# A fixed order for the out-projection's products, transfers at 310 bytes a ns in the planner's table, and all splits on VectorE

## The chip, the cores and the metric

One core of a Trainium2 chip runs the whole program. The metric is device time in microseconds (us), less is better, as the median of several runs. TensorE (PE) multiplies into PSUM, VectorE (DVE), ScalarE (ACT) and GpSimd (POOL) do the rest, SyncE (SP) issues the transfers.

## The reference, cut to what matters

Two layers over 512 tokens of width 1024, in float32. Layer 0 uses stick-breaking attention, layer 1 forgetting attention; both end in a gated feed-forward part.

```python
# layer 0
a = rmsnorm(h, sb_pre_g)
q, k, v = jnp.split(a @ sb_w_qkv, 3, axis=-1)
o = stick_breaking_attention(q, k, v)              # 16 heads of 64
h = h + rmsnorm(merge_heads(o) @ sb_w_o, sb_post_g)    # out-projection
f = conv_ffn(rmsnorm(h, ffn_pre_g), w_up, conv_w, conv_b, w_down)
h = h + rmsnorm(f, ffn_post_g)
# layer 1: the same with forgetting_attention, w_kvf, fox_w_q, fox_w_o
```

`conv_ffn` multiplies by `w_up` (1024 x 5632), convolves three tokens deep, gates, and multiplies by `w_down` (2816 x 1024).

## The kernel before, in words

Every float32 product is made of three: each operand is split into a high part that TensorE takes as it is (`hi`, `AH`) and the rest (`lo`, `AL`), and `AH*hi`, `AH*lo` and `AL*hi` are added in PSUM. A weight tile arrives in `raw` (two buffers), ScalarE writes `whi` (L380) and VectorE `wlo = raw - whi` in two halves (L384); there are eight buffers of each. Three of the eight row tiles of each out-projection weight (`POOL_ROWS`) have their `wlo` made by GpSimd.

Attention goes through eight pairs of heads. A head's scores go to PSUM banks 0 to 2; in layer 0 ScalarE and VectorE then take an Exp (L666), a minimum (L667), two masks (L644, L646), a Ln (L669), a running sum (L670), an Exp (L671) and a product (L672). TensorE transposes the result (L680), ScalarE and VectorE split it into `PH` and `PL` (L686, L687), and TensorE multiplies it with V (L692). The sum goes into `oT` (L701, L702). When both heads of pair p are done, `AH[:, p]` (L720) and `AL[:, p]` (L721) are made of it, `AL` on GpSimd for p under 4 and on VectorE above.

The out-projection (`unit`, L733) has 32 units (b, k), of a block b of 128 tokens and a pair k, with six products each. Block 0 adds up in banks 4 and 5, block 1 in 0 and 1, block 2 in 2 and 3, block 3 in 6 and 7. Units with k = 7 need the last head of all. When a block is complete, `post_block` and `pre_block` normalise it (`mixed`): Square on ScalarE (L465), two small steps on GpSimd (L442, L443), a multiplication by a gain `g` and an update of H on VectorE (L466, L468), again Square (L449), the two small steps, the scaled copy `t` (L454), eight transposes on TensorE (L457), and the split into `AH` (L459) and `AL` (L460). Only then can the first product of the feed-forward part (L436) read that block; it takes tokens 0 to 255, so blocks 0 and 1, for its first three pairs of weight tiles, and the other half after that. At the start of the program `pre_block` does the same for the input.

The order on each engine isn't the order of the code. `Order.pin` records all instructions with what they depend on, `Order.schedule` walks through them by a table of costs (a list schedule: an engine that is free takes the ready instruction with the lowest rank), and the outcome is fixed with dependencies. The code gives an instruction's rank (its place in the program, less `AHEAD` where it reads or writes PSUM, plus `BEHIND` for the splits of weights), so TensorE's products of the out-projection go wherever the planner thinks that they are ready. A transfer in that table takes 520 ns to issue, 1300 ns to start, its bytes at 200 a ns on a wire that all share, and 800 ns to land. SyncE's own order is the program's.

## Time and profile before

| | us |
|---|---|
| median of 3 runs | 1281.49 (1281.36 to 1285.04) |
| the profiled execution's own time | 1283.62 |
| its span in the profile | 1281.8 |
| TensorE busy in the span | 1240.6 |
| VectorE, ScalarE, GpSimd busy | 812.4, 649.4, 103.5 |

The profile follows one execution. The 1.8 us between its own time and its span lie before the first and behind the last instruction. "Busy" is a sum over the whole span; the stretches in which TensorE waits, or gets a lower clock, are read from the rows below.

### The profile page before, as it was taken

The page shows a single profiled execution, that of the slowest core. Times are in us where ns is not written, and L with a number is a line of the kernel's source. Part 1 is how long each engine was busy: PE and PEld are TensorE (multiplying, and loading weights), DVE is VectorE, ACT ScalarE, POOL GpSimd, SP SyncE. Part 2 cuts the span into 40 slices and gives each one's busy share as a digit, 9 for nine tenths or more (in the row PEclk, how much of TensorE's full clock was granted, in tenths as well). Part 3 has the DMA queues.
Part 4 walks back from the last instruction along what each step waited for, and adds up shares of the span by engine and source line. Part 5 has one row for each costly group of instructions (what it writes and reads, how often), then busy time and mean ns, then how long its engine had stood idle before and what let it go on. Part 6 is the DMA issues. An engine that isn't in the chain of part 4 may idle for free.

```text
span 1281.8 us, 16749 instructions
## 1 busy us (share of the span) xinstructions
PE 1240.6 (97%) x6485; PEld 1061.9 (83%) x6485; DVE 812.4 (63%) x1304; ACT 649.4 (51%) x1085; POOL 103.5 (8%) x163
## 2 busy tenths in 40 slices
PE   6999999979999999999998999999899999999998
PEld 5898887869888888888897988978798888888886
DVE  5799999467655555433477888872775555554323
ACT  4688777445433333323477888772553333333221
POOL 1000003020000000000001221241200000000001
PEclk9999999989999999999999999999899999999999
DMA  5313222124433333333221122132343333333301
GB/s 171 98 51 102 79 67 66 50 66 135 129 99 99 99 95 94 93 98 99 66 69 50 34 66 75 58 99 66 99 134 114 99 95 93 95 97 99 99 33 66
DMA packets 145927, 111.97 MB, mean 87 GB/s; under 512 B 4680, under 2 KB 136120, under 8 KB 145848
## 3 DMA queue, kind: packets, MB, share of 16 engines
q1 hardware_dynamic: 145848, 110.90, 29.1%
q8 instruction: 51, 0.84, 0.3%
q14 instruction: 28, 0.23, 0.1%
HBM read 108.79 MB, written 2.10 MB: 87 GB/s over the span
## 4 chain that ended last, share of the span: by engine, by line
PE 86%; DVE 9%; ACT 2%; issue 2%; POOL 0%; DVEq 0%; POOLq 0%; ACTq 0%
PE PS L436 49%; PE PS L733 23%; PE PS L614 6%; PE PS L692 3%; PE PS L680 2%; PE PS L634 2%; DVE ec L670 1%; PE PS L457 1%; DVE wlo L384 1%; DVE PL L687 1%; DVE ec L672 1%; DVE t L454 1%; DVE QS L585 1%; DVE t L466 0%; DVE ec L667 0%
## 5 line engine op out<-in xcount | busy, mean ns | idle before, releaser
L436 PE MATMUL PS<-AH,whi 128*128 128x512 f32 (+1 forms) x1088 | 400.4, 368 | 5.8 <-DVE QS L585 3.1
L436 PE MATMUL PS<-AL,whi 128*128 128x512 f32 (+1 forms) x1088 | 400.9, 369 | 1.1 <-DVE AL L460 1.1
L436 PE MATMUL PS<-AH,wlo 128*128 128x512 f32 (+1 forms) x1088 | 400.1, 368 | 0.0
L384 DVE TENSOR_TENSOR wlo<-raw,whi 128x512 fp32r<-128x512 f32 x332 | 216.7, 690 | 211.4 <-ACT whi L380 210.9
L380 ACT CAST whi<-raw 128x1024 fp32r<-128x1024 f32 x172 | 180.1, 1050 | 197.5 <-PE PS L436 167.4
L436 PEld LDWEIGHTS PS<-AH,whi 128*128 128x128 f32 x1088 | 207.9, 191 | 37.7 <-DVE QS L585 3.2
L436 PEld LDWEIGHTS PS<-AL,whi 128*128 128x128 f32 x1088 | 207.8, 191 | 33.1 <-DVE AL L460 1.7
L436 PEld LDWEIGHTS PS<-AH,wlo 128*128 128x128 f32 x1088 | 207.6, 191 | 31.3
L794 DVE SCALAR_TENSOR_TENSOR hc<-PS,cw,hc 128x511 f32<-128x511 f32 (+1 forms) x176 | 131.3, 746 | 8.6 <-ACT hc L792 5.5
L733 PE MATMUL PS<-whi,ah 128*128 128x512 f32 x352 | 109.3, 390 | 0.0
L733 PE MATMUL PS<-whi,al 128*128 128x512 f32 x352 | 109.1, 389 | 0.0
L733 PE MATMUL PS<-wlo,ah 128*128 128x512 f32 x352 | 108.9, 389 | 0.0
L817 DVE TENSOR_TENSOR al<-act,ah 128x512 fp32r<-128x512 f32 x44 | 30.4, 691 | 116.6 <-ACT ah L816 116.6
L816 ACT CAST ah<-act 128x512 fp32r<-128x512 f32 x44 | 27.4, 623 | 146.2 <-PE PS L733 138.2
L733 PEld LDWEIGHTS PS<-whi,al 128*128 128x128 f32 x352 | 66.1, 188 | 13.7
L733 PEld LDWEIGHTS PS<-wlo,ah 128*128 128x128 f32 x352 | 66.1, 188 | 13.7
L733 PEld LDWEIGHTS PS<-whi,ah 128*128 128x128 f32 x352 | 65.9, 188 | 13.7
L614 PE MATMUL PS<-whi,AH 128*128 128x256 f32 x256 | 73.5, 288 | 3.1 <-ACT whi L380 3.1
L442 POOL TENSOR_SCALAR ss<-ss 128x1 f32<-128x1 f32 x31 | 12.0, 387 | 781.2 <-ACT junk L465 721.4
L614 PE MATMUL PS<-wlo,AH 128*128 128x256 f32 x256 | 73.9, 289 | 0.0
L614 PE MATMUL PS<-whi,AL 128*128 128x256 f32 x256 | 73.3, 287 | 0.0
L792 ACT ACTIVATE hc<-PS,cw 128x512 f32<-128x512 f32 x88 | 68.1, 774 | 8.4 <-PE PS L436 8.3
(132 smaller groups left out, 1740.7 us busy)
## 6 DMA issues: line engine op xcount, KB each, us to landing
raw<-w_up_dram SPq DMA_DIRECT2D x88, 512.0 KB, 3.8
raw<-w_down_dram SPq DMA_DIRECT2D x44, 512.0 KB, 3.6
raw<-sb_w_qkv_dram SPq DMA_DIRECT2D x24, 512.0 KB, 3.7
raw<-w_kvf_dram SPq DMA_DIRECT2D x16, 512.0 KB, 3.7
raw<-sb_w_o_dram SPq DMA_DIRECT2D x8, 512.0 KB, 3.5
raw<-fox_w_q_dram SPq DMA_DIRECT2D x8, 512.0 KB, 3.6
raw<-fox_w_o_dram SPq DMA_DIRECT2D x8, 512.0 KB, 3.6
H<-x_dram SPq DMA_DIRECT2D x4, 512.0 KB, 8.3
```

Source lines behind the costliest of these rows:

```text
L380: order.move(nc.scalar.copy(hi, raw), BEHIND)
L384: order.move(eng.tensor_tensor(out=fl[:, s], in0=fr[:, s], in1=fh[:, s], op=ALU.subtract), BEHIND)
L436: nc.tensor.matmul(ps, a[:, k, :m], b[:, k, t0:t1], start=i == 0, stop=i == n - 1)
L614: nc.tensor.matmul(ps[:, o], a[:, k, sl], m[:, k % 4, :], start=i == 0, stop=i == 3 * KT - 1)
L634: nc.tensor.matmul(z[:, ZOFF[b] : ZOFF[b] + n], a[:, b * P : (b + 1) * P], m[:, :n], start=i == 0, stop=i == len(passes) - 1,)
L680: nc.tensor.transpose(zt[:, o : o + P], E[:, ZOFF[b] + j * P : ZOFF[b] + (j + 1) * P], ident)
L692: nc.tensor.matmul(av[:, j * P :], V[:, j, hh, :], m[:, o : o + n], start=i == 0, stop=i == 7,)
L733: nc.tensor.matmul(y[:, c, :], s[:, sl], m[:, 0, c * 512 : (c + 1) * 512], start=k == 0 and i == 0, stop=k == n - 1 and i == 2,)
L792: nc.scalar.activation(hc, y[:, i, :], AF.Identity, scale=col[:, 2:3], bias=col[:, 3:4])
L794: nc.vector.scalar_tensor_tensor(out=hc[:, s:], in0=y[:, i, : T - s], scalar=col[:, 2 - s : 3 - s], in1=hc[:, s:], op0=ALU.mult, op1=ALU.add,)
L816: nc.scalar.copy(ah, act[:, k, :])
L817: nc.vector.tensor_tensor(out=al, in0=act[:, k, :], in1=f32(ah), op=ALU.subtract)
```

## The change: what it does

1. The out-projection's units get a fixed order by extra dependencies among TensorE's instructions (`Order.after`): units (0, 0..5), (1, 0..3), (0, 6), then (1, 4) no sooner than the last transpose of the last head, (1, 5) no sooner than its last product with V, then (1, 6), (1, 7), (0, 7), and then blocks 2 and 3 whole. Block 1 is complete before block 0. The units held to the end of the down-projection are chained in the same way.
2. The planner's table for a transfer: 310 bytes a ns in place of 200, 700 ns to land in place of 800; the start is 1300 as before.
3. `POOL_ROWS` is gone: VectorE makes every `wlo`, and every `AL` of an attention output.

```diff
-POOL_ROWS = (1, 5, 7)
+FILL = (4, 5)
...
-    ISSUE, FLIGHT, BYTES = 520, 2100, 200.0
+    ISSUE, LEAD, LAND, BYTES = 520, 1300, 700, 310.0
...
+    def after(self, later, earlier):
+        self.turns += [(b.ins.name, a.ins.name) for b in later for a in earlier]
...
+        at = {i.name: n for n, i in enumerate(prog)}
+        for b, a in self.turns:
+            preds[at[b]].setdefault(at[a], 2)
...
-                wire = max(wire, t + 1300) + done - self.FLIGHT
-                end = wire + 800
+                wire = max(wire, t + self.LEAD) + done
+                end = wire + self.LAND
...
-    stream += [row_tile(sb_w_o[0], k, nc.gpsimd if k in POOL_ROWS else nc.vector) for k in range(KT)]
+    stream += [row_tile(sb_w_o[0], k) for k in range(KT)]
...
-                (nc.gpsimd if p < 4 else nc.vector).tensor_tensor(
+                nc.vector.tensor_tensor(
...
-    def out_proj(done):
+    def out_proj(done, heads_end):
         w = {}
-        for b in range(NB):
-            for k in range(KT):
-                if k not in w:
-                    w[k] = take()
-                unit(b, k, KT, (AH[:, k, :], AL[:, k, :]), w[k])
-            done(b)
+        one = [(1, k) for k in range(KT)]
+        steps = [(0, k) for k in range(KT - 2)] + one[: FILL[0]] + [(0, KT - 2), heads_end[0]]
+        steps += one[FILL[0] : FILL[1]] + [heads_end[1]] + one[FILL[1] :]
+        steps += [(0, KT - 1)] + [(b, k) for b in (2, 3) for k in range(KT)]
+        before = []
+        for step in steps:
+            if not isinstance(step, tuple):
+                before.append(step)
+                continue
+            b, k = step
+            if k not in w:
+                w[k] = take()
+            mms = unit(b, k, KT, (AH[:, k, :], AL[:, k, :]), w[k])
+            order.after(mms, before)
+            before = mms[-1:]
+            if k == KT - 1:
+                done(b)
```

Since the planner lays out the whole program, other places move too. Lines 733, 721, 384, 454, 457 and 670 of the kernel before are 742, 730, 392, 462, 465 and 678 in the changed one. Three places:

**TensorE, the end of layer 0's out-projection, before.** `whi24` to `whi31` are the row tiles for k = 0 to 7; `t4` is the normalised block that is transposed. The six `whi31` products in a row are of blocks 0, 1 and 2, the last three rows ahead of the transposes are unit (3, 7):

```order
L733 MATMUL PS_67<-whi27_1819,AH_82 128x512 x2
L733 MATMUL PS_67<-wlo27_1820,AH_82 128x512
L733 MATMUL PS_67<-whi31_2240,AH_82 128x512 x6
L733 MATMUL PS_67<-wlo31_2241,AH_82 128x512
...
L733 MATMUL PS_67<-whi31_2240,AH_82 128x512 x2
L733 MATMUL PS_67<-wlo31_2241,AH_82 128x512 x2
L733 MATMUL PS_67<-whi31_2240,AL_83 128x512 x2
L457 MATMUL PS_67<-ident_68,t4_2343 128x128 x8
L457 MATMUL PS_67<-ident_68,t4_2413 128x128 x8
```

and the same end in the changed kernel: the first three rows are unit (0, 7), the fourth begins unit (2, 0); below the gap stand products of the units (2, 3) and (2, 4) with the transposes of block 1 among them:

```order
L742 MATMUL PS_67<-whi31_2240,AH_82 128x512 x2
L742 MATMUL PS_67<-wlo31_2241,AH_82 128x512 x2
L742 MATMUL PS_67<-whi31_2240,AL_83 128x512 x2
L742 MATMUL PS_67<-whi24_1553,AH_82 128x512 x2
...
L742 MATMUL PS_67<-whi27_1819,AL_83 128x512 x2
L742 MATMUL PS_67<-whi28_1826,AH_82 128x512 x2
L465 MATMUL PS_67<-ident_68,t4_2385 128x128 x8
L742 MATMUL PS_67<-wlo28_1827,AH_82 128x512 x2
```

Before, blocks 0, 1 and 2 become complete together, 27 products of block 3 ahead of the first transposes, with both first transposes at the very end. Now 32 products stand between the last one of block 1 and its transposes, 47 between the last of block 0 and its own, and the transposes of blocks 1, 0 and 2 stand among products of blocks 2 and 3. Layer 1 has the same rows with other numbers.

**VectorE, the last heads of layer 0, before**, from the second mask of head 13 (`ec_2069`, of 0 to 15) to the running sum of head 14 (`ec_2121`):

```order
L646 TENSOR_TENSOR ec_2069<-ec_2069,mask_a_73 128x128
L384 TENSOR_TENSOR wlo30_2026<-raw30_2024,whi30_2025 128x512 x2
L670 SCALAR_TENSOR_TENSOR ec_2070<-R_243,ec_2070 128x1280
L667 TENSOR_SCALAR ec_2120<-ec_2120 128x1280
L644 TENSOR_TENSOR ec_2120<-ec_2120,mask_a_73 128x3x128
L646 TENSOR_TENSOR ec_2120<-ec_2120,mask_a_73 128x128
L672 TENSOR_TENSOR ec_2069<-ec_2069,ec_2070 128x1280
L670 SCALAR_TENSOR_TENSOR ec_2121<-R_243,ec_2121 128x1280
```

and in the changed kernel:

```order
L654 TENSOR_TENSOR ec_2069<-ec_2069,mask_a_73 128x128
L730 TENSOR_TENSOR AL_83<-oT_236,AH_82 128x512
L710 TENSOR_TENSOR oT_236<-PS_67,ot_1984 64x512
L392 TENSOR_TENSOR wlo30_2026<-raw30_2024,whi30_2025 128x512
L678 SCALAR_TENSOR_TENSOR ec_2070<-R_243,ec_2070 128x1280
L675 TENSOR_SCALAR ec_2120<-ec_2120 128x1280
L652 TENSOR_TENSOR ec_2120<-ec_2120,mask_a_73 128x3x128
L654 TENSOR_TENSOR ec_2120<-ec_2120,mask_a_73 128x128
L730 TENSOR_TENSOR AL_83<-oT_236,AH_82 128x512
L680 TENSOR_TENSOR ec_2069<-ec_2069,ec_2070 128x1280
L678 SCALAR_TENSOR_TENSOR ec_2121<-R_243,ec_2121 128x1280
```

Two of the moved `AL` stand ahead of the running sum and of the product of head 13, and one half of `wlo30` has moved behind them.

**TensorE at the start of the program, before** (`whi0`, `wlo0` are the first weight tile, `t4_129` and `t4_145` the first two blocks of the input):

```order
L457 MATMUL PS_67<-ident_68,t4_129 128x128 x8
L614 MATMUL PS_67<-whi0_100,AH_82 128x256
L457 MATMUL PS_67<-ident_68,t4_145 128x128 x8
L614 MATMUL PS_67<-wlo0_101,AH_82 128x256
L614 MATMUL PS_67<-whi0_100,AL_83 128x256
```

and now:

```order
L465 MATMUL PS_67<-ident_68,t4_129 128x128 x8
L465 MATMUL PS_67<-ident_68,t4_145 128x128 x8
L622 MATMUL PS_67<-whi0_100,AH_82 128x256
L622 MATMUL PS_67<-wlo0_101,AH_82 128x256
L622 MATMUL PS_67<-whi0_100,AL_83 128x256
```

The transposes of the second block have moved ahead of the first product; on ScalarE the Square of the second block has moved ahead of the first block's split, and on VectorE the second `t` ahead of the first `AL`. SyncE's order is the same but for one swap of neighbours in each layer; the order within the feed-forward parts and at the end of the program is the same.

## Rows read from the trace of the kernel before

**Rows 1.** The page, part 1: busy us (share of the span) and instructions.
```profile
PE 1240.6 (97%) x6485; PEld 1061.9 (83%) x6485; DVE 812.4 (63%) x1304; ACT 649.4 (51%) x1085; POOL 103.5 (8%) x163
```

**Rows 2.** Waits of TensorE, whole span: us in total, times, longest.
```profile
PE PS L457 <- DVE t L454: 17.2, 5, 8.4
```

**Rows 3.** Timeline of TensorE, layer 0: start, us, instruction, [idle before, releaser].
```profile
268.91 1.06 PE L457 MATMUL PS<-ident,t 128*128 128x128 f32 x8 [0.46 <-DVE t L454]
274.87 1.97 PE L457 MATMUL PS<-ident,t 128*128 128x128 f32 x8 [4.90 <-DVE t L454]
277.94 0.79 PE L436 MATMUL PS<-AH,whi 128*128 128x256 f32 x2 [1.10 <-ACT AH L459]
279.20 0.58 PE L436 MATMUL PS<-AL,whi 128*128 128x256 f32 x1 [0.47 <-DVE AL L460]
```

**Rows 4.** Timeline of TensorE, the same place in layer 1.
```profile
906.88 1.09 PE L457 MATMUL PS<-ident,t 128*128 128x128 f32 x8 [2.64 <-DVE t L454]
909.07 0.78 PE L436 MATMUL PS<-AH,whi 128*128 128x256 f32 x2 [1.10 <-ACT AH L459]
910.53 0.58 PE L436 MATMUL PS<-AL,whi 128*128 128x256 f32 x1 [0.68 <-DVE AL L460]
```

**Rows 5.** Windows: length; busy of PE, PEld, DVE, ACT, POOL; PEclk, DMA share, GB/s.
```profile
225.00:230.00 5.00, 5.00 (x20) 4.58 (x19) 4.19 (x7) 3.66 (x6) 0.00 (x0) 0.51 0.00 0
275.00:280.00 5.00, 3.43 (x13) 2.74 (x14) 4.31 (x5) 3.03 (x5) 1.39 (x3) 0.50 0.34 100
280.00:285.00 5.00, 5.00 (x28) 5.00 (x27) 4.57 (x5) 1.08 (x3) 1.79 (x3) 0.55 0.62 177
910.00:915.00 5.00, 4.47 (x21) 4.47 (x21) 4.45 (x6) 2.63 (x5) 3.16 (x4) 0.50 0.35 104
```

**Rows 6.** Timelines of ScalarE and VectorE: block 0's first Square and its `t`.
```profile
261.51 1.02 ACT L465 ACTIVATE junk<-PS 128x1024 bf16<-128x1024 f32 x1 [5.57 <-PE PS L733]
267.48 1.28 DVE L454 SCALAR_TENSOR_TENSOR t<-H,ss,g 128x1024 f32<-128x1024 f32 x1 [2.19 <-POOL ss L443]
```

**Rows 7.** Chain of waits, merged pieces: start, us, what.
```profile
254.85 6.59 PE PS L733 x29
291.11 9.00 PE PS L436 x75
```

**Rows 8.** Timeline of VectorE in layer 0's last heads.
```profile
201.29 2.07 DVE L672 TENSOR_TENSOR ec<-ec 128x1280 f32<-128x1280 f32 x1 [0.18 <-ACT ec L671]
218.67 1.48 DVE L672 TENSOR_TENSOR ec<-ec 128x1280 f32<-128x1280 f32 x1
220.09 2.83 DVE L670 TENSOR_TENSOR_SCAN ec<-R,ec 128x1280 f32<-128x1280 bf16 x1
```

**Rows 9.** Timeline of GpSimd in layer 0's last heads.
```profile
201.97 6.72 POOL L721 TENSOR_TENSOR AL<-oT,AH 128x512 fp32r<-128x512 f32 x4
```

**Rows 10.** Line 721 on VectorE: count, ns min/median/max, first and last start.
```profile
L721 DVE TENSOR_TENSOR AL<-oT,AH x8: 681/693/1617, 205.9 to 878.0; 128x512 fp32r<-128x512 f32 x8
```

**Rows 11.** Timeline of TensorE in layer 0's last heads.
```profile
220.21 1.09 PE L680 MATMUL PS<-ident,ec 128*128 128x128 f32 x8 [0.89 <-DVE ec L672]
223.70 0.79 PE L692 MATMUL PS<-PL,V 128*128 128x512 f32 x1 [1.66 <-DVE PL L687]
```

**Rows 12.** Timelines of ScalarE and TensorE at the start of the program.
```profile
5.00 1.06 ACT L449 ACTIVATE junk<-H 128x1024 bf16<-128x1024 f32 x1 [2.94 <-DMA H<-x_dram]
10.44 1.01 ACT L459 CAST AH<-PS 128x1024 fp32r<-128x1024 f32 x1 [4.29 <-PE PS L457]
11.35 1.06 ACT L449 ACTIVATE junk<-H 128x1024 bf16<-128x1024 f32 x1
16.41 0.56 PE L614 MATMUL PS<-wlo,AH 128*128 128x256 f32 x1
```

**Rows 13.** The page, part 6: transfers, count, KB each, median us to landing.
```profile
raw<-w_up_dram SPq DMA_DIRECT2D x88, 512.0 KB, 3.8
H<-x_dram SPq DMA_DIRECT2D x4, 512.0 KB, 8.3
```

More of the change, by code (lines that the diff above doesn't have):

```diff
@@ L58, in __init__ @@
         self.shift = {}
+        self.turns = []
         self.old = {i.name for i in self.nc.all_instructions()}
@@ L111, in cost @@
         if op == "DMACopy":
-            return self.ISSUE, self.FLIGHT + n * o[0].ap[0][1] * 4 / self.BYTES
+            return self.ISSUE, n * o[0].ap[0][1] * 4 / self.BYTES
         if op == "LoadActFuncSet":
@@ L422, in tile_trunk @@
             stream += qk if pr else qk + v if g else v + qk
-    stream += [row_tile(fox_w_o[0], k, nc.gpsimd if k in POOL_ROWS else nc.vector) for k in range(KT)]
+    stream += [row_tile(fox_w_o[0], k) for k in range(KT)]
     stream += ffn_stream(1)
@@ L679, in head @@
                     for b in range(j, NB):
-                        nc.tensor.transpose(
+                        tr = nc.tensor.transpose(
                             zt[:, o : o + P], E[:, ZOFF[b] + j * P : ZOFF[b] + (j + 1) * P], ident
@@ L691, in head @@
                     for m in (PH, PL):
-                        nc.tensor.matmul(
+                        mm = nc.tensor.matmul(
                             av[:, j * P :], V[:, j, hh, :], m[:, o : o + n],
@@ L702, in head @@
             nc.vector.tensor_tensor(out=self.oT[s, p, :], in0=av[s], in1=ot[s], op=ALU.add)
+            return tr, mm
         def run(self):
@@ L715, in run @@
                     self.project(p + 1)
-                self.head(p, 1)
+                end = self.head(p, 1)
                 if p % 2 and p + 1 < NPAIR:
@@ L720, in run @@
                 nc.scalar.copy(AH[:, p, :], self.oT[:, p, :])
-                (nc.gpsimd if p < 4 else nc.vector).tensor_tensor(
+                nc.vector.tensor_tensor(
                     out=AL[:, p, :], in0=self.oT[:, p, :], in1=f32(AH[:, p, :]), op=ALU.subtract
                 )
+            return end
     def unit(b, k, n, a, w, cols=(0, 1)):
@@ L730, in unit @@
         hi, lo = w
-        for i, (s, m) in enumerate(((ah, hi), (ah, lo), (al, hi))):
-            for c in cols:
-                nc.tensor.matmul(
-                    y[:, c, :], s[:, sl], m[:, 0, c * 512 : (c + 1) * 512],
-                    start=k == 0 and i == 0, stop=k == n - 1 and i == 2,
-                )
+        return [
+            nc.tensor.matmul(
+                y[:, c, :], s[:, sl], m[:, 0, c * 512 : (c + 1) * 512],
+                start=k == 0 and i == 0, stop=k == n - 1 and i == 2,
+            )
+            for i, (s, m) in enumerate(((ah, hi), (ah, lo), (al, hi)))
+            for c in cols
+        ]
     def flat_pair(i):
         return pair_of(i).rearrange("p a c -> p (a c)")
-    def out_proj(done):
+    def out_proj(done, heads_end):
         w = {}
-        for b in range(NB):
-            for k in range(KT):
-                if k not in w:
-                    w[k] = take()
-                unit(b, k, KT, (AH[:, k, :], AL[:, k, :]), w[k])
-            done(b)
+        one = [(1, k) for k in range(KT)]
[15 more added lines that the diff above has]
+                done(b)
     def down_proj(lhs, done, final, last=4):
@@ L758, in down_proj @@
             for b in (0, 2, 3, 1):
-                unit(b, k, NC, a, w)
+                end = unit(b, k, NC, a, w)[-1:]
         for b in range(NB):
@@ L762, in down_proj, with ffn_phase @@
                 for k, a, w in held:
-                    unit(b, k, NC, a, w, cols)
+                    mms = unit(b, k, NC, a, w, cols)
+                    order.after(mms, end)
+                end = mms[-1:]
             done(b)
-    def ffn_phase(l, post_g, next_g, final):
+    def ffn_phase(l, heads_end, post_g, next_g, final):
         with tc.tile_pool(name=f"ffn{l}", bufs=2) as pool:
@@ L776, in mixed @@
                 pre_block(b, g2, t4, junk)
-            out_proj(mixed)
+            out_proj(mixed, heads_end)
             act = pool.tile([P, NC, T], F32, name="act", bufs=1)
@@ L883, in tile_trunk @@
         act_table("natural_log_exp_and_others")
-        Attn(pool, False).run()
-    ffn_phase(0, sb_post_g[0], None, False)
+        end = Attn(pool, False).run()
+    ffn_phase(0, end, sb_post_g[0], None, False)
     with tc.tile_pool(name="attn1", bufs=2) as pool:
@@ L890, in tile_trunk @@
         act_table("natural_log_exp_and_others")
-        Attn(pool, True).run()
-    ffn_phase(1, fox_post_g[0], None, True)
+        end = Attn(pool, True).run()
+    ffn_phase(1, end, fox_post_g[0], None, True)
     order.pin(PS, ("Exp", "Ln", "Gelu_apprx_tanh"))
```

## The prediction

> **What bounds the kernel now.** I read the busy times first: TensorE works in 97% of the span [rows 1], so a gain can come only from the 41 us in which it stands still, and from stretches in which it works at the lower clock. The waits of TensorE come next: one line leads them, the transposes of a normalised block that wait for `t` (L457 for L454), 17.2 us in five waits, 8.4 of them at the start of the program [rows 2]. The timeline shows where the others are: at the end of layer 0's out-projection TensorE waits 0.46, 4.90, 1.10 and 0.47 us, 6.93 together [rows 3]; at the same place in layer 1 2.64, 1.10 and 0.68, 4.42 together [rows 4]. Last the windows, for the clock: around these waits the granted clock is 0.50 to 0.55, the level of 1.2 GHz [rows 5]. At 275 to 285 us TensorE is busy for 3.43 us wholly at that level, and of the next 5.00 for 0.9 (a mean of 0.55 is nine tenths at a half): 7.9 us, half of which, 4.0, is lost. In layer 1 4.47 us at 0.50 lose 2.2. So the two places cost 10.9 and 6.6 us.
>
> Why they wait: block 0's chain from its first Square to the last wait before its transposes takes 261.51 to 268.76, 7.3 us [rows 6], and the next blocks queue on the same ScalarE and VectorE. One product of the out-projection takes 6.59 / 29 = 0.227 us at the full clock [rows 7]. Before, blocks 0 to 2 become complete together with 27 products left, 6.1 us of cover for chains that need 7.3 for the first block and more for the second.
>
> **The change, part by part.**
>
> *The fixed order.* Block 1 is complete 32 products, 7.3 us, ahead of its transposes, which is its chain to the tenth; block 0 has 47 products and eight transposes (1.06 us, [rows 3]), 11.7 us. Its update of H and its second Square stand behind block 1's, by my count of the steps in between some 4 us behind: 7.3 + 4 = 11.3. Block 2 has 38 products behind the transposes of block 0, 8.6 us, and block 3 69 products of 256 columns at 9.00 / 75 = 0.12 us [rows 7], 8.3. So each of the four is covered with nothing to spare, and I allow 1.5 us of new waits in each layer (bounds: 0, and 5 where a chain is late; see the second rival). Worth: 10.9 - 1.5 = 9.4 us in layer 0, 6.6 - 1.5 = 5.1 in layer 1. The weights of the feed-forward part don't get in the way: their buffers come free with the units (3, k), 1.36 us each, and TensorE takes 24 x 0.12 = 2.9 us for each of the first tiles, while a transfer lands in 3.8 [rows 13].
>
> *What this order takes from the last heads.* Units of block 1 that filled the time between the last head's transposes and its products with V are now held for later. In layer 0 three products with V follow those transposes with nothing between, and in layer 1 this is so for head 14. A wait of that form (V for `PL`) is 1.66 us where it stands now [rows 11]. I take 1.0 in each layer, between 0 and 1.66 and nearer the upper, since here no running sum stands ahead of the `PL`.
>
> *The splits on VectorE.* Six halves of `wlo` and four `AL` more in each layer, at 0.69 us [rows 10]: 6.9 us of VectorE work in each, at most. None of it need lie on the path. Between the products (L672) of heads 12 and 13 start to start took 218.67 - 201.29 = 17.4 us [rows 8]. In the changed order 20 instructions stand between these two: one running sum of 2.83 [rows 8] and 19 others, most of them 512 wide, a few wider and a few narrower; at 0.69 each that is 13.1, and with the first product itself at 1.48, as its sibling takes, 17.4 us. Three `AL` more fit since VectorE was slowed or waiting before: the first of these products took 2.07, an `AL` up to 1.62 [rows 8, 10], while GpSimd was at its four `AL` for 6.72 us [rows 9]. With these gone, and a half of `wlo30` moved behind, the transposes of head 13 that waited 0.89 for that product [rows 11] should wait less. I book +0.9 gain and the 1.0 us of loss from above against each other in layer 0: 0, with bounds of 2 us of gain (what the collisions cost) and 6.9 of loss. In layer 1 the 1.0 stays as a loss, with bounds 0 and 6.9.
>
> How much the collision costs is a place to weigh a rule. The two rows differ by 2.07 - 1.48 = 0.59 us. The Trainium skill, in "SBUF — State Buffer", section "SBUF: two separate sides", says that VectorE and GpSimd share a pair of ports by an exclusive lock, so that the one that comes second waits for the other's whole instruction. A GpSimd `AL` is 6.72 / 4 = 1.68 us long, so by that rule each collision could give back 1.68 in place of 0.59. The row shows less than the rule; the sum goes by the row.
>
> *The transfers.* The table changes no transfer. It moves the planner's idea of 512 KB from 1.3 + 2.6 + 0.8 = 4.7 us to 1.3 + 1.7 + 0.7 = 3.7, where the profile has 3.8 [rows 13]. The one place that matters is the start. There the second block's Square stood on ScalarE behind the first block's split, at 11.35 [rows 12], and the block's transposes came between the first product and the rest, which began at 16.41. Now that Square goes ahead of the split. When its data lands isn't shown. If at once, the transposes run straight behind the first ones, which end at 10.4; split and cast then end at about 12.5, the transposes (1.97) likewise, and the stream begins some 3.3 us earlier after the one product that it had done. If as late as 11.35, the split ends 2.2 later than now, and the stream begins some 1.3 later. The first block is read at 5.0 [rows 12], and the transfers of H that the profile can time land after 8.3 us [rows 13]; this one is issued between, so I put it near 8, and take 2.0 gained.
>
> Sum: 9.4 + 5.1 + 0 - 1.0 + 2.0 = 15.5 us. From the profiled execution's own 1283.62 that gives 1268.1. That execution is 2.1 us above the median of the runs; I take 1268, which leaves 13.5 against the median.
>
> **The rivals.**
>
> *First: the last heads give half of it back.* The gain at the transition stands, but VectorE's extra work and the missing filler make TensorE wait a few us in the last heads, and the clock falls there too. For it: 0.89 and 1.66 us of waits there now are followed by 0.51 of the clock at 225 to 230 [rows 5, 11], which cost 2.4 us; VectorE was busy for 4.19 of those 5. Against it: the count of 17.4 above. Price: 2.5 us of waits and 2.4 of clock in each layer, 9.8: 1278 to 1268 + 4.9 = 1273 where one layer pays. The Trainium skill speaks for this one: "TensorE: Matmul & The Clock Gate", section "A second HAM failure mode: psum-queue depth-cycling", has a TensorE with short idle times between groups of products fall back to half clock again and again. Here such idle times stand in each of these places; the row that bears on it is the 0.51 above, so the trace agrees for waits of 2.5 us, and shows nothing for less.
>
> *Second: the chain is late for another reason.* `g`, the gain that block 1's first multiplication reads, can be loaded only when the attention's buffers are given up, behind the last `AL`. By the order that multiplication comes some 4 us behind it. A transfer lands in 3.8, or in 8.3 where many are under way [rows 13]. At 8.3 block 1's transposes come 4.3 us late, and the old wait is back, with the clock: 5 to 7 us in each layer, 1278 to 1282, or 1274 in one alone. Against it: SyncE has little to do there.
>
> *Third: nothing is gained.* The planner's cover is undone by the actual times, and the gain stays within 0.3%, 3.8 us, which is about what these runs can tell from no change: above 1277.6. It is the first two at their upper ends.
>
> *Fourth, slower: VectorE becomes the bound of the last heads.* All 6.9 us of added work in each layer lie on the path, with 2.4 of clock: 18.6 us against 15.5 + 1.0 gained: 1286. It decides from the point at which the product of head 13 starts later than TensorE's fill reaches, which is now, by 0.89 us; what speaks against it is that collisions and a half tile leave the same stretch.
>
> **How the numbers follow.** The forecast, 1262 to 1272, has 0.58. The first rival, 1272 to 1278, has 0.24; the second 0.08, the third 0.05, the fourth 0.05. The low end is all gains at their better bounds: 15.5, 3.0 for waits that don't come, 1.3 at the start, 2.0 and 1.0 in the last heads, 22.8 below 1283.6, so 1260; the high end takes in the first rival whole: 1278. Outside lie the third and fourth and part of the second, and a little below. Faster by over 0.3%: the forecast, the first rival, and half of the second, 0.86; slower 0.05; the rest 0.09.
>
> **What would show it.** The waits of the transposes (now L465) for `t`, outside the start, should fall from 8.0 us to under 3, and the windows around the end of each out-projection should have a clock of 1.00. GpSimd should lose some 30 us (20 instructions of up to 1.68), VectorE gain some 12. The first product's stream should begin at about 14.4. The products of heads 13 and 14 should start no more than 1 us later, counted from that of head 12. Wrong would be: a clock of 0.5 at the last heads of both layers (first rival), a wait of block 1's first multiplication for its `g` (second), an idle time of TensorE there that VectorE ends (fourth).

## The result and the profile after

The changed kernel takes 1275.77 us (1272.74 to 1276.23, five runs) against 1281.51 for the one before; the ratio is 0.9939, 95% interval 0.9922 to 0.9956. That is 5.7 us, where 13.5 were forecast. The profiled execution took 1275.78 us, 7.8 less than the 1283.62 of before.

The page, part 1, answers to [rows 1]:

```profile
PE 1239.4 (97%) x6485; PEld 1058.1 (83%) x6485; DVE 820.7 (64%) x1324; ACT 651.0 (51%) x1085; POOL 74.3 (6%) x143
```

GpSimd lost 29.2 us and VectorE gained 8.3, and TensorE has as much to do as before. The waits of TensorE come next, as in [rows 2] (the longest in total, some rows left out where the dots stand):

```profile
PE PS L465 <- DVE t L462: 11.3, 6, 8.0
...
PE PS L688 <- POOL ec L668: 2.2, 4, 1.1
PE PS L700 <- DVE PL L695: 1.9, 3, 1.4
...
PE PS L642 <- ACT KH L603: 1.6, 1, 1.6
...
```

Outside the start the waits for `t` are down to 0.49 + 0.38 + 0.38 = 1.25 us (8.0 before [rows 2]), and below them stands a list of small ones from the heads. The timeline of TensorE shows where both are (start, us, instruction, [idle before, releaser]): the start, the last heads and the transition of layer 0, and those of layer 1.

```profile
13.05 0.56 PE L622 MATMUL PS<-whi,AH 128*128 128x256 f32 x1
...
44.21 0.62 PE L642 MATMUL PS<-KH,QS 128*128 128x512 f32 x2 [1.63 <-ACT KH L603]
...
223.05 0.56 PE L700 MATMUL PS<-PL,V 128*128 128x512 f32 x1 [1.44 <-DVE PL L695]
...
237.07 1.09 PE L688 MATMUL PS<-ident,ec 128*128 128x128 f32 x8 [1.12 <-DVE ec L680]
...
254.28 1.06 PE L465 MATMUL PS<-ident,t 128*128 128x128 f32 x8 [0.49 <-DVE t L462]
...
270.29 1.09 PE L465 MATMUL PS<-ident,t 128*128 128x128 f32 x8 [0.38 <-DVE t L462]
...
857.20 1.72 PE L688 MATMUL PS<-ident,ec 128*128 128x128 f32 x8 [1.10 <-POOL ec L668]
...
864.04 0.50 PE L742 MATMUL PS<-whi,AH 128*128 128x512 f32 x1 [1.15 <-ACT ec L662]
...
885.90 1.07 PE L465 MATMUL PS<-ident,t 128*128 128x128 f32 x8 [0.18 <-issue]
...
901.96 1.09 PE L465 MATMUL PS<-ident,t 128*128 128x128 f32 x8 [0.38 <-DVE t L462]
```

Where [rows 3] had 6.93 us of waits at the end of layer 0's out-projection there are 0.49 and 0.38, and where [rows 4] had 4.42 there are 0.18 and 0.38. The windows (columns as in [rows 5]) give the clock at the same places:

```profile
45.00:50.00 5.00, 4.90 (x17) 4.05 (x17) 2.00 (x4) 2.40 (x4) 0.00 (x0) 0.66 0.38 116
220.00:225.00 5.00, 3.32 (x17) 2.60 (x16) 5.00 (x5) 2.95 (x5) 0.00 (x0) 0.83 0.00 0
225.00:230.00 5.00, 5.00 (x25) 4.00 (x25) 4.48 (x9) 3.08 (x5) 0.00 (x0) 0.82 0.00 0
250.00:255.00 5.00, 4.51 (x24) 3.57 (x23) 2.81 (x3) 2.27 (x4) 2.34 (x4) 1.00 0.11 31
270.00:275.00 5.00, 4.71 (x30) 4.25 (x31) 2.77 (x5) 3.58 (x4) 0.00 (x0) 1.00 0.50 146
855.00:860.00 5.00, 3.52 (x17) 2.07 (x15) 4.22 (x9) 3.31 (x7) 1.68 (x3) 0.82 0.02 5
860.00:865.00 5.00, 3.85 (x16) 3.15 (x17) 2.60 (x6) 2.68 (x10) 0.00 (x0) 0.84 0.00 0
900.00:905.00 5.00, 4.62 (x26) 3.63 (x25) 2.33 (x3) 1.91 (x2) 0.59 (x1) 1.00 0.72 210
```

At both transitions (250 to 275 and 900 to 905) it is 1.00, where [rows 5] had 0.50 and 0.55. But it falls at 45 us and in the last heads of layer 1, where it did not before. In the last heads of layer 0 it is 0.83 and 0.82, which is better than the 0.80 and 0.51 of the same windows before.

To see what each place gave or took I compared, in the profiled executions, the times at which TensorE had the same share of its work behind it (each product weighed with its time at full clock, 0.227 us for 512 columns and less for narrower ones). How the narrow ones are weighed moves a single entry by up to 1 us, and the rows add up to the differences of the profiled times within 0.4. The table has, for each kernel told of here, the us gained on the kernel before in each stretch; the stretches are in the time of the kernel before. The first column is the time of the profiled execution, the second the ratio of the timed runs. "T" is the new table, "S" the splits on VectorE, "O" the fixed order.

| kernel | profiled, us | ratio | 0 to 37 | first heads, to 204 | last heads 0, to 266 | transition 0, to 288 | to 809 | last heads 1, to 896 | transition 1, to 926 | rest |
|---|---|---|---|---|---|---|---|---|---|---|
| O, T, S (the change) | 1275.78 | 0.9939 | 4.0 | -4.1 | -2.7 | 10.5 | -1.9 | -6.0 | 7.9 | 0.4 |
| O (order_only) | 1278.49 | 0.9938 | 0.5 | -0.3 | -3.6 | 10.5 | -1.7 | -8.1 | 7.5 | 0.2 |
| T (table_only) | 1283.83 | 1.0016 | 4.0 | -3.1 | 0.6 | 0.9 | -0.6 | -2.8 | 0.5 | 0.3 |
| S (splits_only) | 1282.81 | 0.9997 | 0.5 | 1.1 | 0.2 | 1.2 | -0.2 | -2.4 | 0.6 | 0.2 |
| T, S (no_order) | 1275.17 | 0.9942 | 4.0 | -2.8 | 1.8 | 1.4 | -0.8 | -2.4 | 7.0 | 0.5 |
| O, T (no_splits) | 1280.12 | 0.9942 | 3.2 | -3.7 | -4.4 | 10.5 | -1.8 | -8.0 | 7.5 | 0.3 |
| O, S (no_table) | 1273.72 | 0.9931 | -0.3 | 1.7 | -5.0 | 10.5 | -0.5 | -3.8 | 7.6 | 0.0 |
| O in layer 0, T, S (l0_order) | 1270.12 | 0.9904 | 4.0 | -1.1 | -2.7 | 10.5 | -0.9 | -2.1 | 6.6 | -0.6 |
| O with (5, 6), T, S (fill56) | 1272.55 | 0.9927 | 3.4 | -0.6 | -2.1 | 10.5 | -1.2 | -6.3 | 7.6 | -0.1 |
| block 3 last, T, S (b3_last) | 1272.42 | 0.9934 | 3.9 | -1.1 | 0.7 | 4.9 | -1.1 | -2.8 | 7.4 | -0.6 |
| block 3 last (b3_only) | 1272.76 | 0.9932 | -1.1 | -0.1 | 0.5 | 7.6 | 0.2 | 0.3 | 3.4 | 0.0 |
| O in layer 0, T at 280, S (l0_t280) | 1267.91 | 0.9893 | 4.4 | 0.8 | -4.0 | 10.5 | -0.5 | -1.3 | 6.5 | -0.3 |
| block 3 last, T at 280 (b3_t280) | 1274.43 | 0.9938 | 4.5 | -0.3 | -0.1 | 5.1 | 0.0 | -2.2 | 1.8 | 0.3 |

For the change the row reads: the transitions gave 10.5 and 7.9, more than forecast, the start gave 4.0, and of that 8.7 us went in the last heads of the two layers, 4.1 in the first heads and 1.9 on the way to the last heads of layer 1, where the clock at 685 to 695 us is 0.50 and 0.90 (0.75 and 1.00 in the kernel before at 695 to 705).

One execution stands behind each row, and part of these losses is its own. Up to 208 us the change, no_order, l0_order, fill56 and b3_last run the same instructions in the same order on TensorE, ScalarE and VectorE, and yet their first heads read -4.1, -2.8, -1.1, -0.6 and -1.1. The change and l0_order have the same order up to 839 us, and up to 809 they read -1.9 and -0.9. Differences of that size in these columns tell nothing of an edit. The profiled executions of order_only and no_splits are 2.8 and 4.7 us above the medians of their runs; in no_splits the clock is 0.53 and 0.50 at 860 to 870 us, so the 8 us lost there are the high end.

### The profile page after: what moved, and what is told of

Read it like the earlier page. It is cut to its first block, busy times and chain, and to the rows that moved or that the text cites. A ratio compares the mean times of both kernels' runs of the same rounds, so it can differ in the third digit from the quotient of the medians.

```text
span 1274.1 us, 16766 instructions
## 1 busy us (share of the span) xinstructions
PE 1239.4 (97%) x6485; PEld 1058.1 (83%) x6485; DVE 820.7 (64%) x1324; ACT 651.0 (51%) x1085; POOL 74.3 (6%) x143
## 4 chain that ended last, share of the span: by engine, by line
PE 80%; DVE 13%; ACT 3%; DMA 1%; POOL 1%; issue 1%; DVEq 0%; SPq 0%; POOLq 0%; ACTq 0%
PE PS L444 47%; PE PS L742 21%; PE PS L622 5%; PE PS L700 3%; DVE ec L678 2%; PE PS L688 2%; PE PS L642 2%; DVE PL L695 1%; DVE wlo L392 1%; DVE ec L680 1%; PE PS L465 1%; DVE t L462 1%; DVE QS L593 1%; DVE ec L675 1%; DVE H L476 1%
## 5 line engine op out<-in xcount | busy, mean ns | idle before, releaser
L392 DVE TENSOR_TENSOR wlo<-raw,whi 128x512 fp32r<-128x512 f32 x344 | 223.8, 688 | 197.4 <-ACT whi L388 196.9
L742 PEld LDWEIGHTS PS<-whi,ah 128*128 128x128 f32 x352 | 65.9, 188 | 13.5
L825 ACT ACTIVATE hc<-hc 128x512 f32<-128x512 f32 x44 | 27.8, 631 | 84.9 <-DVE hc L820 84.9
```

The source lines that it names most:

```text
L392: order.move(eng.tensor_tensor(out=fl[:, s], in0=fr[:, s], in1=fh[:, s], op=ALU.subtract), BEHIND)
L742: nc.tensor.matmul(y[:, c, :], s[:, sl], m[:, 0, c * 512 : (c + 1) * 512], start=k == 0 and i == 0, stop=k == n - 1 and i == 2,)
L825: nc.scalar.activation(hs[0], hs[0], AF.Gelu_apprx_tanh)
```

## The experiments

My theory after the result: the parts add up; the order is worth the transitions, the table costs some at the start, and the last heads lose to the units that the order holds back. The first rival was that the table is neutral, the second that VectorE's extra work is what the last heads pay for.

**Without the table.**

```diff
-    ISSUE, LEAD, LAND, BYTES = 520, 1300, 700, 310.0
+    ISSUE, LEAD, LAND, BYTES = 520, 1300, 800, 200.0
```

> The changed kernel with the planner's old table for transfers (200 bytes a ns, 800 ns to land); fixed order and VectorE splits kept. Theory (the table costs more than it brings): the start falls back by 4.0 us, but the 1.63 us wait for KH at 44 us and the clock of 0.66 behind it go, which gives 4.7 back, and the start of the second attention gives up to 1.4 more: 1271 to 1275. Rival (whatever the start gains is eaten by the first heads, so the table is neutral by 60 us): 1275.8 within 1 us, and the wait at 44 us takes another form. Second rival (the table pays): 1279 or more.

Measured: 1274.47 us, ratio to before 0.9931 (0.9915 to 0.9947), which overlaps that of the change. The start falls back (-0.3 in place of 4.0) and the first heads gain 1.7 in place of losing 4.1. By 204 us it is 1.5 us ahead of the change, which is within what the first heads vary by in one and the same order; the last heads of layer 0 take that back. The time fits the theory's range and, within the interval, the rival; what the wait at 44 us is made of shows in the ScalarE timeline of the changed kernel:

```profile
38.42 1.05 ACT L388 CAST whi<-raw 128x1024 fp32r<-128x1024 f32 x1 [1.17 <-DMA raw<-sb_w_qkv_dram]
41.92 1.05 ACT L388 CAST whi<-raw 128x1024 fp32r<-128x1024 f32 x1 [2.45 <-DMA raw<-sb_w_qkv_dram]
42.99 0.58 ACT L602 CAST KH<-PS 64x512 fp32r<-64x512 f32 x1
43.58 0.58 ACT L603 CAST KH<-PS 64x512 fp32r<-64x512 f32 x1
```

ScalarE stands 2.45 us for a transfer, and the two casts of KH that the next scores need stand behind that cast. With the old table those casts stand ahead of it, so the new one put it in front, and the transfer came too late for that. How much later differs from one execution to the next: in kernels of the same order ScalarE waits 0.87 us (fill56) to 2.97 (no_order) for it, and TensorE not at all to 2.07 for KH.

**Without the order.**

```diff
...
-        steps = [(0, k) for k in range(KT - 2)] + one[: FILL[0]] + [(0, KT - 2), heads_end[0]]
...
+        steps = [(b, k) for b in range(NB) for k in range(KT)]
...
-            order.after(mms, before)
-            before = mms[-1:]
...
-                    order.after(mms, end)
```

> The changed kernel without the fixed order (units in the planner's own order again); table and VectorE splits kept. Theory (the order is worth 10.3 us at the end of layer 0's out-projection and 7.9 in layer 1, and costs some of the 2.4 and 4.0 us lost in the last heads): 1275.8 + 18.2 - 3 = 1291, between 1288 and 1294, with waits of TensorE for t and a clock near 0.5 at both transitions. Rival (the VectorE splits alone, by taking GpSimd's part of the chain away, shorten the transitions): under 1285, waits for t under 5 us.

Measured: 1275.64 us, 0.9942 (0.9930 to 0.9954). The theory is wrong: the time is that of the change, and yet layer 0's transition still waits. Both signs of the rival came (a time under 1285, and 3.80 us of waits for `t` outside the start), but not its cause: the splits alone, told of below, free no transition. TensorE's timeline of this kernel:

```profile
44.57 0.62 PE L642 MATMUL PS<-KH,QS 128*128 128x512 f32 x2 [2.07 <-ACT KH L603]
...
269.99 1.97 PE L465 MATMUL PS<-ident,t 128*128 128x128 f32 x8 [3.80 <-DVE t L462]
...
894.02 1.06 PE L465 MATMUL PS<-ident,t 128*128 128x128 f32 x8 [0.19 <-issue]
...
903.68 0.39 PE L444 MATMUL PS<-AL,whi 128*128 128x256 f32 x1 [0.26 <-DVE AL L468]
```

In layer 1 the stall is gone without any fixed order (0.19 and 0.26), and the last heads lose 3.6 us less there than in the change, and 4.5 less in layer 0. So the parts do not add up.

**Without the splits, and the order alone.**

```diff
-    stream += [row_tile(sb_w_o[0], k) for k in range(KT)]
+    stream += [row_tile(sb_w_o[0], k, nc.gpsimd if k in (1, 5, 7) else nc.vector) for k in range(KT)]
...
-                nc.vector.tensor_tensor(
+                (nc.gpsimd if p < 4 else nc.vector).tensor_tensor(
```

> The changed kernel with the 12 halves of wlo and the 8 AL back on GpSimd; fixed order and table kept. Theory (the losses in the last heads, 2.4 us in layer 0 and 4.0 in layer 1, come from the units that the order holds back, not from the VectorE splits): 1275.8 within 1.5, the same waits near 223, 237, 857 and 864 us. Rival (the added 6.9 us of VectorE in each layer is what the last heads pay for): 1270 to 1273 and shorter waits there. Second rival (GpSimd slows VectorE by collisions and is late itself): 1278 or more.

> The kernel before with the fixed order alone (old table, GpSimd splits). Theory (all of the gain is the order's): 1281.5 - 18.2 + 3 to 6 for the last heads = 1266 to 1270, so faster than the changed kernel, since the table's losses at the start and in the second attention are not there. Rival (the order needs the splits on VectorE to be on time): 1275 or more.

Measured: 1275.39 us, 0.9942 (0.9927 to 0.9957), and 1275.66 us, 0.9938 (0.9925 to 0.9950). Beside the fixed order the splits are worth nothing that the runs can tell, and they don't cost anything either: the rival of the added 6.9 us on VectorE is out. The order alone has the whole gain of the change, but not the 1266 to 1270 of my theory, since the last heads lose more than I had put in. The time is that of its rival (1275 or more), whose cause falls all the same: with GpSimd's splits the transitions gain as much (10.5 and 7.5), so the order does not need the others to be on time.

**The table alone, the splits alone.** The same edits, taken one at a time from the kernel before.

> The kernel before with the new table alone (planner's own order, GpSimd splits). The run without the fixed order lost nothing at layer 1's transition (waits of 0.19 and 0.26 us where the kernel before has 4.42), so table or splits took that stall away. Theory (the splits did, since GpSimd's AL no longer hold back its part of the last heads): here the three waits near 900 us stay at 4 us or more, and the time is 1279 to 1282. Rival (the table did, by another order of the casts): waits there under 1 us, 1274 to 1277. In both the start's 4 us should be gone by 140 us.

> The kernel before with the 20 instructions moved from GpSimd to VectorE alone (planner's own order, old table). Theory (the splits free layer 1's transition): waits under 1 us at its end, a gain of some 6.6 us there and of 2 in layer 0's last heads: 1273 to 1276. Rival (the table did it): the waits of 4 us stay, 1279 to 1282.

Measured: 1284.30 us, 1.0016 (1.0006 to 1.0025), and 1282.35 us, 0.9997 (0.9988 to 1.0006). Neither theory nor rival: the stall at 907 us stays with either, and only both together take it away. The table alone makes the kernel 0.16% slower, an interval clear of 1. In the table's case VectorE's timeline shows what holds block 1's `t` (start 905.72); the same stretch of the kernel with block 3 last, told of below, stands under it:

```profile
902.78 1.89 DVE L392 TENSOR_TENSOR wlo<-raw,whi 128x512 fp32r<-128x512 f32 x3
904.59 1.22 DVE L474 TENSOR_TENSOR t<-PS,g 128x1024 f32<-128x1024 f32 x1
905.72 1.28 DVE L462 SCALAR_TENSOR_TENSOR t<-H,ss,g 128x1024 f32<-128x1024 f32 x1
```

```profile
894.11 1.22 DVE L468 TENSOR_TENSOR AL<-PS,AH 128x1024 fp32r<-128x1024 f32 x1
895.25 0.69 DVE L392 TENSOR_TENSOR wlo<-raw,whi 128x512 fp32r<-128x512 f32 x1
895.86 1.27 DVE L462 SCALAR_TENSOR_TENSOR t<-H,ss,g 128x1024 f32<-128x1024 f32 x1
```

Behind the `AL` of the block ahead stand three halves of `wlo` and the next block's multiplication in the first, one half in the second. I read this so: with the new table blocks 0 to 2 are complete earlier, but it also plans the feed-forward weights earlier, and their splits come in between. What the splits on VectorE add to it, so that both together free the transition, no run here takes apart.

**The order in layer 0 only.**

```diff
-            order.after(mms, before)
+            if fixed:
+                order.after(mms, before)
...
-            out_proj(mixed, heads_end)
+            out_proj(mixed, heads_end, l == 0)
```

> The changed kernel with the fixed order in layer 0 only; in layer 1 the units go by the planner's own order, as in the run without the fixed order. Theory (in layer 1 the order buys nothing that the other two parts don't give already, and costs 4 us in the last heads): 1275.8 - 4 = 1271 to 1273. Rival (the 4 us there are a clock that happened to fall in the one profiled run): 1275 to 1277.

Measured: 1270.55 us, 0.9904 (0.9890 to 0.9918), the interval clear of the change's. The theory holds in sign: in layer 1 the order takes 3.9 us of the last heads (-6.0 against -2.1) and gives 1.3 at the transition, 2.6 together. It does not explain the 5.2 us between the medians: 4.0 of the profiled difference lie ahead of 809 us, where both kernels run the same order. Against the change's two faster runs (1272.74 and 1273.08, told of at the end) the median here is 2.4 us less, which is about what layer 1 gives.

**One unit more ahead of the last transposes.**

```diff
-FILL = (4, 5)
+FILL = (5, 6)
```

> The changed kernel with one unit of block 1 more ahead of the last head's transposes and one less behind its last product with V, in both layers (six products, 1.36 us). Block 1 is complete with the same 32 products behind it, so the transitions should not change. Theory (the held units are what the last heads miss): the 1.12 us wait of the last transposes in layer 0 goes, and one of 1.1 in layer 1: 1275.8 - 2.4 = 1272.5 to 1274. Rival (the waits only move to the next product): 1275 to 1276.5.

Measured: 1273.68 us, 0.9927 (0.9913 to 0.9941), overlapping the change's interval. In the table the last heads gain 0.6 and lose 0.3: the rival. The 1.12 us of the last transposes in layer 0 are gone, and a little later TensorE waits for the cast of a row tile, in this kernel's timeline:

```profile
241.87 0.73 PE L742 MATMUL PS<-whi,AH 128*128 128x512 f32 x2 [0.93 <-ACT whi L388]
```

In layer 1 the planner put the last transposes behind the same products as in the change, so there the edit tested nothing. The 3.5 us between the first heads of the two profiled executions are not the edit's either: the order there is the same, and the clock did not fall in this one.

**Block 3 last.** What O alone and T with S have in common is that pair 7's units of blocks 0 to 2 come ahead of more of block 3. So this constraint alone takes the place of the fixed order (whose lines go as in "Without the order"), once with T and S and once in the kernel before:

```diff
+            if (b, k) == (2, KT - 1):
+                before = mms[-1:]
+            if b == 3:
+                order.after(mms, before)
```

> The changed kernel without its fixed order; in its place one constraint, that no unit of block 3 comes ahead of the last unit of block 2. Only layer 0 is altered by it (seven products of block 3 stood ahead there; in layer 1 none did). Theory (the transition waits where units of block 3 run before blocks 0 to 2 are complete: they use up the cover, and the weight buffers they free put splits of the next weights into the chain): TensorE may wait up to 1.6 us for the units of pair 7, and the waits of 3.80, 1.10 and 0.46 us at the end shrink by more than that, to under 2 together: 1275.6 - 3 to 6 = 1270 to 1273. Rival (the time from the last AL to the end is all that counts, and the order of the rest is the same): the wait only moves ahead of pair 7 and is longer by the clock, 1275 to 1278.

> The kernel before with that one constraint alone (old table, GpSimd splits, no fixed order). 21 products of block 3 stood ahead in layer 0 and 10 in layer 1, so TensorE waits up to 4.8 and 2.3 us for pair 7 if their data come no earlier. Theory (pair 7 must be ready early too, which is what table and splits give together): the stall moves ahead of pair 7 and little is gained, 1279 to 1283. Rival (the place of block 3 alone decides): 1272 to 1276.

Measured: 1273.28 us, 0.9934 (0.9921 to 0.9948), and 1273.45 us, 0.9932 (0.9919 to 0.9945). With T and S the change is small, between theory and rival, and the waits at the end shrink by 1.4 us only, not to under 2. In the kernel before, the rival is right and my theory wrong: these four lines alone gain as much as the change does. They needed no earlier data, because the data were there. Rows of the kernel before, GpSimd and then TensorE: its last `AL`, on VectorE, had ended at 246.65 us, its last half of `wlo` for pair 7 ends at 246.95 + 2.53 = 249.48, and the six first products that read pair 7's tile start at 258.09, 8.6 us later. In layer 1 it is 881.51 and 890.09, 8.6 us again.

```profile
246.95 2.53 POOL L384 TENSOR_TENSOR wlo<-raw,whi 128x512 fp32r<-128x512 f32 x2 [38.26 <-ACT whi L380]
```

```profile
258.09 1.52 PE L733 MATMUL PS<-whi,AH 128*128 128x512 f32 x6
```

With block 3 last they move 21 products, 4.8 us, ahead, no wait comes in front of them, and the transition of layer 0 in that kernel is:

```profile
264.17 1.06 PE L465 MATMUL PS<-ident,t 128*128 128x128 f32 x8 [0.23 <-DVE t L462]
270.14 1.09 PE L465 MATMUL PS<-ident,t 128*128 128x128 f32 x8 [0.34 <-DVE t L462]
272.33 0.50 PE L444 MATMUL PS<-AH,whi 128*128 128x256 f32 x2 [1.10 <-ACT AH L467]
273.79 0.38 PE L444 MATMUL PS<-AL,whi 128*128 128x256 f32 x1 [0.96 <-DVE AL L468]
```

So the stall of 4.90 us is gone, and the waits for block 1's split behind it (1.10 and 0.96) stay; in the change there is none there but 0.38 us for `t`. In layer 1 the same two stay, and the clock at 900 to 905 us is 0.66: there this kernel gains 3.4 us and the change 7.9. It makes up for that in the last heads, from which it takes no filler (0.5 and 0.3 against -2.7 and -6.0).

The planner had filled the time ahead of pair 7 with block 3, which was the cover of the transition. That it did so because by its table and costs the data came later than they did is my reading; its own times are not shown.

**280 bytes a ns.** Once with the order in layer 0, T and S, and once with nothing but block 3 last in the kernel before (there from 200 and 800):

```diff
-    ISSUE, LEAD, LAND, BYTES = 520, 1300, 700, 310.0
+    ISSUE, LEAD, LAND, BYTES = 520, 1300, 700, 280.0
```

> The changed kernel with the fixed order in layer 0 only and 280 bytes a ns in the table. At the start one cast of a weight whose transfer was late (the ScalarE waited 1.81 us for it at 41 us) then stands behind the first KH and no longer ahead of it. Theory (that cast made the wait of TensorE for KH at 43 us): the wait of 0.76 to 2.07 us goes, 0.5 to 1.5 us faster than with 310: 1269 to 1270.5. Rival (the first heads are bound by VectorE, and what TensorE gains there is lost by 80 us): the same as with 310, 1270.5 within 0.7.

> The kernel before with the constraint on block 3 and a table of 280 bytes a ns and 700 ns to land; no fixed order, GpSimd splits as before. Theory (the place of block 3's units frees both transitions, the table's 280 keeps the 4 us of the start, and neither the held units nor the moved splits are needed): 1273.45 - 4 = 1268 to 1270.5, as fast as the version with the fixed order in layer 0 and 280. Rival (the three parts compete for the same slack: what the start gains is lost in the last heads, where VectorE shares the work with GpSimd's splits): 1271 to 1274.

Measured: 1268.44 us, 0.9893 (0.9879 to 0.9908), the fastest of all; and 1274.57 us, 0.9938 (0.9925 to 0.9952). In the first ScalarE now runs one cast and the first KH ahead of the next:

```profile
38.14 1.05 ACT L388 CAST whi<-raw 128x1024 fp32r<-128x1024 f32 x1 [1.08 <-DMA raw<-sb_w_qkv_dram]
40.12 0.58 ACT L602 CAST KH<-PS 64x512 fp32r<-64x512 f32 x1 [0.94 <-PE PS L444]
40.72 0.58 ACT L603 CAST KH<-PS 64x512 fp32r<-64x512 f32 x1
41.32 1.05 ACT L388 CAST whi<-raw 128x1024 fp32r<-128x1024 f32 x1
```

TensorE does not wait for KH any more (0 to 2.07 us with 310), and the start keeps its 4.4 us through the first heads (0.8 more by 204), so the rival of a bound by VectorE falls. Its interval overlaps that of the run with 310, so the 2 us between them rest on the trace. In the second the start is kept as well, but the transitions give 5.1 and 1.8 in place of 7.6 and 3.4, and the time lies 0.6 us above the rival's range, by another mechanism than it named. With the new table two halves of `wlo` more stand on VectorE between block 0's update of H and its `t`; this kernel first, then the one with block 3 last alone, both in layer 1:

```profile
886.25 1.28 DVE L476 SCALAR_TENSOR_TENSOR H<-t,ss,H 128x1024 f32<-128x1024 f32 x1
887.45 2.49 DVE L392 TENSOR_TENSOR wlo<-raw,whi 128x512 fp32r<-128x512 f32 x4
890.66 1.28 DVE L462 SCALAR_TENSOR_TENSOR t<-H,ss,g 128x1024 f32<-128x1024 f32 x1 [0.72 <-POOL ss L451]
```

```profile
886.30 1.28 DVE L476 SCALAR_TENSOR_TENSOR H<-t,ss,H 128x1024 f32<-128x1024 f32 x1
887.50 1.29 DVE L392 TENSOR_TENSOR wlo<-raw,whi 128x512 fp32r<-128x512 f32 x2
889.78 1.28 DVE L462 SCALAR_TENSOR_TENSOR t<-H,ss,g 128x1024 f32<-128x1024 f32 x1 [1.00 <-POOL ss L451]
```

From the update to that `t` it is 4.41 us in place of 3.48, and in layer 0 the same (4.42 and 3.48). In layer 1 another 0.3 us comes up to block 1's `t`, where ScalarE waits 2.33 us for a transfer ahead of an urgent cast of `AH`; in layer 0 such a wait of 2.13 us adds nothing. TensorE then waits for block 1, in this kernel's timeline (0.38 us in the other kernel):

```profile
898.41 1.90 PE L465 MATMUL PS<-ident,t 128*128 128x128 f32 x8 [1.86 <-DVE t L462]
```

## Why the prediction was right in sign and too large

The forecast was 15.5 us between the profiled executions and it was 7.8. Term by term, as the table has them: 18.4 for the transitions in place of 14.5, 4.0 at the start in place of 2.0, -8.7 in the last heads in place of -1.0, and -4.1 and -1.9 in the first heads and up to 809 us, which I had put at nothing. From 15.5 I took 13.5 for the runs, since I set a forecast that starts from the slower profiled execution against their median; from the median itself it would have been 1266.

*What bounds the kernel, and where the gain can come from*: right. The transitions gave 10.5 and 7.9 us, against 9.4 and 5.1. New waits were 0.87 and 0.56 us in place of the 1.5 that I allowed (the 0.49 and the 0.18 among them stand in the table under the last heads), and in layer 1 the cost had been taken too small: the windows on both sides of the one I counted were at 0.91 as well.

*What this order takes from the last heads*: this step failed, in size. I booked 0 in layer 0 and 1.0 in layer 1; it was 2.7 and 6.0. The runs split it: T and S without the order gain 1.8 there in layer 0, so the order costs 4.5; in layer 1 it costs 3.9, and the other 2.1 are lost without it too. I counted VectorE's work between the products of heads 12 and 13 (17.4 us; it became 218.19 - 202.75 = 15.4, since the 19 narrow instructions took 11.1 in place of 13.1) and took one wait of the form V for `PL`. But VectorE was not late. TensorE has less to do while it waits for the heads: 66 products of the out-projection run ahead of the last of the last head's transposes in layer 0 and 58 in layer 1, where it was 79 and 68, and the waits come at several places: 0.79, 0.24, 1.44, 1.12, 0.24, 0.22 in layer 0, where the kernel before has 0.89, 0.24, 1.66. The time is that of my first rival (1272 to 1278), and so is one of its two causes, the missing filler. The other, VectorE's extra work, is ruled out by the run without the splits, and its sign, a clock of 0.5 in both layers, did not come: the clock fell anew in layer 1 alone, to 0.82 and 0.84. Which of the held products is missed most stays open: one unit more in layer 0 moved the wait and did not remove it.

*The splits on VectorE*: hidden, as booked. The product of head 12 takes 1.49 us in place of 2.07 with GpSimd's work beside it gone, which is the 0.59 of the row; the sum by the row holds. But I had set the price of the lock in the Trainium skill, "SBUF — State Buffer", section "SBUF: two separate sides", too high: who comes second waits for what is left of the other's instruction, and not for 1.68 us whatever it meets. The trace of the kernel before agrees with that. The product began at 201.29, when GpSimd was at a half of `wlo` and not yet at an `AL`, with 0.73 us left; the slow `AL` of [rows 10] met a GpSimd `AL` with 1.07 us left and took 0.93 longer than its siblings (VectorE and GpSimd, start and us):

```profile
200.72 1.30 POOL L384 TENSOR_TENSOR wlo<-raw,whi 128x512 fp32r<-128x512 f32 x1
```

```profile
205.94 1.62 DVE L721 TENSOR_TENSOR AL<-oT,AH 128x512 fp32r<-128x512 f32 x1
```

```profile
205.72 1.29 POOL L721 TENSOR_TENSOR AL<-oT,AH 128x512 fp32r<-128x512 f32 x1
```

Beside the fixed order the splits changed no time: with and without them the runs are the same. Without it they did, together with the table (0.9942 against 1.0016 for the table alone). GpSimd's 29.2 us less are the 30 of the forecast, VectorE's 8.3 more are under its 12.

*The transfers*: the step was right as far as it went and stopped too early. The stream began at 13.05 us, ahead of the 14.4 that I took, and the start gave 4.0 in place of 2.0. I followed the table no further than the first products, and wrote that only the start matters. The same table put casts of late transfers ahead of KH, and by 204 us the gain was gone: -4.1, of which the clock at 45 to 50 us is 0.34 x 5 = 1.7. Other executions of the same order lost 0.6 to 2.8 there, so this one was among the bad ones.

*The second rival*, a late `g`, did not come: the waits of block 1's transposes are 0.49 and 0.18 us. *The third and fourth* did not either.

What I did not think of at all is that the gain had several keys. Any of the fixed order, table and splits together, or four lines on block 3 gives 0.993 to 0.994, and the change's three parts are not worth more than the first of them. They come to the same time by different sums: at the transitions the order alone gains 18.0 us, table and splits 8.4 and block 3 last 11.0, and in the last heads they lose 11.7, lose 0.6 and gain 0.8. That they meet at nearly one time is chance as far as the runs show, and the order in layer 0 alone, with T and S, does better than any of them (0.9904).

## What to carry to other kernels

When a planner's order leaves a stall, compare when an operand was ready in the trace with when it was used: here pair 7 lay ready for 8.6 us, and letting the filler go behind it was worth as much as writing out the whole order. A planner's table by which transfers land sooner than they do costs through the engine that splits them in a fixed order: look for a wait on a transfer with urgent work queued behind it. Price a fixed order at the places from which it takes the filler, and test parts of a change alone and in pairs before adding their gains up.

## What the runs showed of the hardware

A wait of the same form at the same place brought the clock down in one execution and not in another. After the 1.63 us at 44 us it was 0.66 in the changed kernel; after 1.64 us, without the splits, and after 2.07 us, without the order, it stayed at full (the latter's window):

```profile
45.00:50.00 5.00, 4.91 (x25) 3.95 (x24) 2.60 (x5) 3.64 (x5) 0.00 (x0) 1.00 0.34 106
```

The five runs of the changed kernel fall in two groups: 1272.7 and 1273.1 us at a mean clock of 0.997, 1275.8 to 1276.2 at 0.992 and 0.993. The profiled execution is of the second; at which places the first group kept its clock isn't shown. The Trainium skill's "TensorE: Matmul & The Clock Gate", section "A second HAM failure mode: psum-queue depth-cycling", has short idle times between groups of products bring the clock down again and again; the rows agree that waits of 1 to 2 us can do it (0.82 and 0.84 at 855 to 865 us), and show that they need not. So a gain that consists of such waits comes with a spread of some 3 us a run here, and the ranges for this kernel have to hold it.

The transfers of `sb_w_qkv`, 512 KB each, land in 3.7 us by the median of the changed kernel. One of them took 5.9 us from its issue at 35.98 to the cast that waited for it at 41.92. The one ahead of it had landed by 38.42, when its cast began, and from 40.5 to 42.0 us the windows show only 18 to 31 GB/s, presumably the rest of it. In l0_order, with the same order up to there, the cast began at 41.01. What delays the rest isn't shown.
